# A row softmax on one core: the row maxima moved into a fallback path, eight larger tiles, two late loads on SyncE's queue

## The chip, the cores and the metric

The kernel runs on one core of one Trainium2 chip. The metric is the device time in microseconds (us) of one execution; before the change its median over 9 runs is 160.14 us (159.97 to 160.28). One execution was also taken by the hardware profiler. Its own time is 160.04 us, and its span, from the first to the last recorded instruction, is 158.7 us; the 1.34 us between the two lie outside what the profile shows.

## What is computed

A softmax with temperature 2 over the last axis of a 16 x 1024 x 512 array of float32:

```python
x_scaled = x / 2.0
x_max = np.max(x_scaled, axis=-1, keepdims=True)
exp_x = np.exp(x_scaled - x_max)
return exp_x / np.sum(exp_x, axis=-1, keepdims=True)
```

There are 16,384 rows of 512 numbers, drawn from a normal distribution. Input and output are 33.55 MB each, and each is moved once. The maximum cancels in the quotient; it is there so that the exponential can't overflow.

## The kernel before

The rows are spread over the 128 partitions of the on-chip memory, so each partition has 128 rows to do. "A row" below means one row in each partition, 262,144 bytes in all. A tile is some rows of every partition; within a tile the rows of one partition lie side by side in the main memory, so that one partition's share of a transfer is one unbroken run (a tile of 15 rows: 30,720 bytes).

The tiles are listed in `PLAN`: 3, 7, 13 and then seven times 15 rows. They live in one arena of 98 rows, in which each is computed in place. The first eight tiles fill it, and the last two (tiles 8 and 9) take the places of earlier ones: tile 8 those of tiles 0, 1 and 2, tile 9 those of tiles 2 and 3. A tile is cut into chunks of 3 to 5 rows, 27 in all.

- **Loads.** Tile 0 goes out on SyncE's queue (L105), tile 1 in three pieces on ScalarE's (L110), both ahead of the start barrier; tiles 2 to 7 follow on ScalarE's queue (L114). Tile 8 is issued by ScalarE after its exponentials of tile 4, tile 9 after those of tile 5 (`AFTER`), each when the stores of the tiles in its place have landed (L189, L190).
- **VectorE** takes the negated maximum of a chunk's rows from the loaded data (L118), and for the chunk two places back (`LAG`) the reciprocal of the row sums (L127) and the multiplication by it. In tiles 1 to 3 (`FUSED`) that is one TENSOR_TENSOR per chunk (L131), otherwise one TENSOR_SCALAR per row (L138).
- **ScalarE** takes exp(0.5 x + bias) row by row, with the row sum as a by-product. The bias is the value that VectorE left in `stats`. The rows of tiles 0 to 5 are written out one by one (L176); those of tiles 6 to 9 run in a loop of 5 rows a turn (L211), which waits on a semaphore that TensorE passes on (L168, L203).
- **SyncE** stores tile after tile (L158), each when its last chunk has been multiplied (L157), and at the end waits for the stores (L162).

Nothing plans the order at run time: each engine follows its own list and waits on semaphores. Transfers of one queue run in the order in which they were issued, and the two queues share the same 16 DMA engines.

Of the kernel before, what the change touches and what calls it, by code (L numbers as in the profile page):

```python
# [6 lines left out]

PLAN = [
    ([3], 0), ([4, 3], 3), ([5, 4, 4], 10), ([5] * 3, 23), ([5] * 3, 38), ([5] * 3, 53),
    ([5] * 3, 68), ([5] * 3, 83), ([5] * 3, 0), ([5] * 3, 15),
]
ARENA = 98
LAG = 2

SPREAD = 1

AFTER = {8: 4, 9: 5}  # L20

FUSED = {1, 2, 3}

LOOP = 6
E = 5


@with_exitstack
def kernel(
# [5 lines left out]
    nc = tc.nc  # L35
    tc.close()
    tc.compile()
    fp32 = mybir.dt.float32

    xf = x.flatten_outer_dims()  # L40
    of = out.flatten_outer_dims()
    N, D = xf.shape
    P = nc.NUM_PARTITIONS
    n_rows = N // P
    assert sum(sum(c) for c, _ in PLAN) == n_rows

    arena = nc.alloc_sbuf_tensor("arena", (P, ARENA, D), fp32)

    stats = nc.alloc_sbuf_tensor("stats", (P, n_rows), fp32)
    recip = nc.alloc_sbuf_tensor("recip", (P, n_rows), fp32)  # L50

    tiles, chunks, base = [], [], 0
    for t, (cs, at) in enumerate(PLAN):
        r = sum(cs)
        tiles.append((base, r, at))
        o = 0
        for c in cs:
            chunks.append((t, base + o, c, at + o))  # L60
            o += c
        base += r
    last_chunk = {c[0]: k for k, c in enumerate(chunks)}

    def dram(ap, t):
        b, r, _ = tiles[t]
        return ap[b * P : (b + r) * P].rearrange("(p r) d -> p r d", r=r)

    def sb(t):
        _, r, at = tiles[t]  # L70
        return arena[:, at : at + r, :]


    behind = {}
    for t, (_, r, at) in enumerate(tiles):
        for u in range(t):
            _, ru, au = tiles[u]
            if at < au + ru and au < at + r:
                behind.setdefault(t, []).append(u)

    ld = [nc.alloc_semaphore(f"ld{t}") for t in range(len(tiles))]
    awaited = sorted({u for us in behind.values() for u in us})


    st, need = {}, {}
    for t in sorted(behind):
        new = [u for u in behind[t] if u not in st]
        sem = nc.alloc_semaphore(f"st{t}")
        st.update({u: sem for u in new})
        need[t] = (sem, 16 * len(new))  # L90
    s_end = nc.alloc_semaphore("s_end")
    s_max = nc.alloc_semaphore("s_max")
    s_exp = nc.alloc_semaphore("s_exp")
    s_go = nc.alloc_semaphore("s_go")
    s_rec = nc.alloc_semaphore("s_rec")
    s_mul = nc.alloc_semaphore("s_mul")

    def issue_loads(begin, end):


        for t in range(begin, end):
            if t in behind:
                continue
            if t == 0:
                nc.sync.dma_start(out=sb(t), in_=dram(xf, t)).then_inc(ld[t], 16)  # L105
            elif t == SPREAD:

                r = tiles[t][1] - 1
                for p, q, lo, hi in ((0, P, 0, r), (0, 126, r, r + 1), (126, P, r, r + 1)):
                    nc.scalar.dma_start(  # L110
                        out=sb(t)[p:q, lo:hi], in_=dram(xf, t)[p:q, lo:hi]
                    ).then_inc(ld[t], 16)
            else:
                nc.scalar.dma_start(out=sb(t), in_=dram(xf, t)).then_inc(ld[t], 16)  # L114

    def do_max(k):
        t, b, c, a = chunks[k]
        nc.vector.reduce_max(  # L118
            out=stats[:, b : b + c],
            in_=arena[:, a : a + c],  # L120
            axis=mybir.AxisListType.X,
            negate=True,
        )._wait_ge(ld[t], 48 if t == SPREAD else 16).then_inc(s_max, 1)

    def do_mul(k):
        t, b, c, a = chunks[k]
        nc.vector.reciprocal(  # L127
            out=recip[:, b : b + c], in_=stats[:, b : b + c]
        )._wait_ge(s_exp, k + 1).then_inc(s_rec, 1)
        if t in FUSED:  # L130
            nc.vector.tensor_mul(  # L131
                out=arena[:, a : a + c],
                in0=arena[:, a : a + c],
                in1=recip[:, b : b + c].unsqueeze(2).to_broadcast([P, c, D]),
            )._wait_ge(s_rec, k + 1).then_inc(s_mul, 1)
            return
        for r in range(c):
            ins = nc.vector.tensor_scalar_mul(  # L138
                out=arena[:, a + r],
                in0=arena[:, a + r],  # L140
                scalar1=recip[:, b + r : b + r + 1],
            )
            if r == 0:
                ins._wait_ge(s_rec, k + 1)
        ins.then_inc(s_mul, 1)

    def compute_and_store():

        for k in range(len(chunks) + LAG):
            if k < len(chunks):  # L150
                do_max(k)
            if k >= LAG:
                do_mul(k - LAG)


        for t in range(len(tiles)):
            nc.sync.wait_ge(s_mul, last_chunk[t] + 1)  # L157
            nc.sync.dma_start(out=dram(of, t), in_=sb(t)).then_inc(  # L158
                st[t] if t in awaited else s_end, 16
            )  # L160

        nc.sync.wait_ge(s_end, 16 * (len(tiles) - len(awaited)))  # L162


        straight = [k for k, c in enumerate(chunks) if c[0] < LOOP]
        loop = [k for k, c in enumerate(chunks) if c[0] >= LOOP]
        for k in loop:
            nc.tensor.wait_ge(s_max, k + 1).then_inc(s_go, 1)  # L168


        nc.scalar.preload_act_table(mybir.ActivationFunctionType.Exp)  # L171
        late = sorted(behind)
        for k in straight:
            t, b, c, a = chunks[k]
            for r in range(c):
                ins = nc.scalar.activation(  # L176
                    out=arena[:, a + r],
                    in_=arena[:, a + r],
                    func=mybir.ActivationFunctionType.Exp,
                    bias=stats[:, b + r : b + r + 1],  # L180
                    scale=0.5,
                    accum_out=stats[:, b + r : b + r + 1],
                )
                if r == 0:
                    ins._wait_ge(s_max, k + 1)
            ins.then_inc(s_exp, 1)
            while late and last_chunk[AFTER[late[0]]] <= k:
                u = late.pop(0)
                nc.scalar.wait_ge(*need[u])  # L189
                nc.scalar.dma_start(out=sb(u), in_=dram(xf, u)).then_inc(ld[u], 16)  # L190
        assert not late


        first = chunks[loop[0]][1]
        assert all(
            c == E and b == first + j * E and a == b % ARENA
            for j, (_, b, c, a) in enumerate(chunks[k] for k in loop)
        )
        row = nc.scalar.alloc_register("row")
        nc.scalar.reg_mov(row, first)  # L200
        with nc.scalar.While(lambda: nc.scalar.snap(row, min_val=first, max_val=n_rows) < n_rows):
            now = nc.scalar.snap(row, min_val=first, max_val=n_rows - E)
            nc.scalar.wait_ge(s_go, 1).then_inc(s_go, -1)  # L203
            at = nc.s_assert_within(
                now % ARENA, 0, ARENA - E,
                skip_runtime_bounds_check_because="no chunk reaches over the arena's end",
            )
            for r in range(E):
                data = arena[:, r : ARENA - E + 1 + r][:, bass.ds(at, 1)]
                stat = stats[:, r : n_rows - E + 1 + r][:, bass.ds(now, 1)]  # L210
                ins = nc.scalar.activation(  # L211
                    out=data,
                    in_=data,
                    func=mybir.ActivationFunctionType.Exp,
                    bias=stat,
                    scale=0.5,
                    accum_out=stat,
                )
            ins.then_inc(s_exp, 1)
            nc.scalar.reg_add(row, row, E)  # L220

    here = str(nc.cur_bb)
    entry, rest = nc.main_func.blocks[0], list(nc.main_func.blocks[1:])
    head, jumps = entry.instructions[:-5], entry.instructions[-5:]
    entry.instructions = []
    nc.switch_bb("main", None)
    issue_loads(0, 2)
    first = list(entry.instructions)  # L230
    at = next(k for k, i in enumerate(head) if type(i).__name__ == "InstDrain")
    entry.instructions = head[:at] + first + head[at:]
    act = []
    entry.instructions = list(entry.instructions) + [i for i in jumps if i not in act]
    nc.switch_body(here, parent=None, valid_engines=[i.engine for i in jumps])
    issue_loads(2, len(tiles))
    compute_and_store()


# [28 lines left out]
```

## Time and profile before

| quantity | value |
|---|---|
| median of 9 runs | 160.14 us |
| the profiled execution: time / span | 160.04 / 158.7 us |
| bytes moved, mean rate over the span | 67.13 MB, 423 GB/s |
| VectorE busy | 131.4 us (83%), 155 instructions |
| ... of it row maxima (L118, 27) | 72.2 us |
| ... of it multiplications (L131, 8 and L138, 93) | 19.9 and 38.6 us |
| ScalarE busy | 94.4 us (59%) |
| last load landed / last store issued / its landing | 127.8 / 147.1 / 158.6 us |

The page of a profile has the busy share of each engine and of the DMA engines in 40 slices of the span, one digit a slice (9 is 90% or more); the DMA queues with their packets, megabytes and the time that their packets took as a share of 16 engines' span; and the chain of waits, which follows the work that ended last back to the start. q1 is SyncE's queue, q10 ScalarE's, and q14 fetches instructions. The view of windows gives for stretches of the span the busy time of VectorE, ScalarE and GpSimd with their instructions, TensorE's clock, the DMA share and the rate. "DVE" is VectorE, "ACT" ScalarE, "POOL" GpSimd and "SP" SyncE. Lines like L118 are those of the kernel's source.

### The profile page before, as it was taken

How to read it: one execution, taken by the hardware profiler on the slowest of the kernel's cores; microseconds unless marked ns; L12 is line 12 of the kernel's file. 1: busy time of each engine (PE TensorE's matmuls, PEld its weight loads, DVE VectorE, ACT ScalarE, POOL GpSimd, SP SyncE). 2: the span in 40 equal slices, each digit the busy share in tenths (PEclk: the TensorE clock that was granted, in tenths of full speed). 3: DMA queues.
4: the chain of work that ended last, by engine and by line, in shares of the span. 5: the costliest groups of instructions: out<-in, count | busy, mean ns of one | idle time of the engine just before them, and what ended most of it. 6: DMA issues, size and time to landing. Idle time of an engine off the chain costs nothing.

```text
span 158.7 us, 621 instructions
## 1 busy us (share of the span) xinstructions
DVE 131.4 (83%) x155; ACT 94.4 (59%) x257; POOL 0.2 (0%) x4
## 2 busy tenths in 40 slices
DVE  0467699999999999999999999996999379999000
ACT  0359297736874684679748786667566809764000
POOL 0000000000000000000000000000000000000000
DMA  7989999999999999999999999999999999999995
GB/s 274 454 362 430 427 415 465 430 386 428 466 454 395 426 463 438 418 443 418 449 418 449 418 449 418 441 426 426 441 418 449 418 449 418 449 418 449 410 457 256
DMA packets 3026, 67.13 MB, mean 423 GB/s; under 512 B 336, under 2 KB 336, under 8 KB 720
## 3 DMA queue, kind: packets, MB, share of 16 engines
q1 hardware_dynamic: 1584, 34.34, 50.5%
q10 hardware_dynamic: 1440, 32.77, 48.5%
q14 instruction: 2, 0.02, 0.0%
HBM read 33.55 MB, written 33.55 MB: 423 GB/s over the span
## 4 chain that ended last, share of the span: by engine, by line
DMA 52%; DVE 38%; issue 0%
DMA arena<-in_x_dram 38%; DVE stats L118 18%; DMA out_dram<-arena 14%; DVE arena L131 13%; DVE arena L138 7%; DVE recip L127 1%
## 5 line engine op out<-in xcount | busy, mean ns | idle before, releaser
L118 DVE TENSOR_REDUCE stats<-arena 128x5 f32<-128x2560 f32 (+2 forms) x27 | 72.2, 2677 | 14.7 <-DMA arena<-in_x_dram 14.7
L176 ACT ACTIVATE arena<-arena,stats 128x512 f32<-128x512 f32 x68 | 48.2, 711 | 23.4 <-DVE stats L118 23.4
L211 ACT ACTIVATE arena<-arena,stats x60 | 42.5, 710 | 20.7 <-ACTq L203 20.7
L138 DVE TENSOR_SCALAR arena<-arena,recip 128x512 f32<-128x512 f32 x93 | 38.6, 483 | 0.7
L131 DVE TENSOR_TENSOR arena<-arena,recip 128x2560 f32<-128x2560 f32 (+2 forms) x8 | 19.9, 2492 | 0.3
L176 ACT ACTIVATION_READ_ACCUMULATOR arena<-arena,stats 128x1 f32 x68 | 12.8, 188 | 0.0
L211 ACT ACTIVATION_READ_ACCUMULATOR arena<-arena,stats x60 | 11.2, 187 | 0.0
L171 ACT ACT_TABLE_LOAD x1 | 1.3, 1283 | 6.0 <-issue 6.0
L127 DVE RECIPROCAL recip<-stats 128x5 f32<-128x5 f32 (+2 forms) x27 | 4.8, 178 | 0.0
L252 POOL MEMSET const-uint8-127<- 128x1 uint8 x1 | 0.1, 102 | 0.0
L252 POOL MEMSET const-bfloat16-1.0<- 128x1 bf16 x1 | 0.1, 101 | 0.0
L252 POOL MEMSET const-float32-0.0<- 128x1 f32 x1 | 0.1, 98 | 0.2 <-issue 0.2
L252 POOL MEMSET const-float32-1.0<- 128x1 f32 x1 | 0.1, 98 | 0.0
## 6 DMA issues: line engine op xcount, KB each, us to landing
arena<-in_x_dram ACTq DMA_DIRECT2D x7, 3840.0 KB, 46.9
out_dram<-arena SPq DMA_DIRECT2D x7, 3840.0 KB, 22.5
arena<-in_x_dram ACTq DMA_DIRECT2D x1, 3328.0 KB, 14.5
out_dram<-arena SPq DMA_DIRECT2D x1, 3328.0 KB, 20.7
out_dram<-arena SPq DMA_DIRECT2D x1, 1792.0 KB, 17.3
arena<-in_x_dram ACTq DMA_DIRECT2D x1, 1536.0 KB
arena<-in_x_dram SPq DMA_DIRECT2D x1, 768.0 KB, 6.2
out_dram<-arena SPq DMA_DIRECT2D x1, 768.0 KB, 15.1
```

The lines of the kernel that those rows point to most:

```text
L118: nc.vector.reduce_max(out=stats[:, b : b + c], in_=arena[:, a : a + c], axis=mybir.AxisListType.X, negate=True,)._wait_ge(ld[t], 48 if t ...
L127: nc.vector.reciprocal(out=recip[:, b : b + c], in_=stats[:, b : b + c])._wait_ge(s_exp, k + 1).then_inc(s_rec, 1)
L131: nc.vector.tensor_mul(out=arena[:, a : a + c], in0=arena[:, a : a + c], in1=recip[:, b : b + c].unsqueeze(2).to_broadcast([P, c, D]),)._w ...
L138: ins = nc.vector.tensor_scalar_mul(out=arena[:, a + r], in0=arena[:, a + r], scalar1=recip[:, b + r : b + r + 1],)
L171: nc.scalar.preload_act_table(mybir.ActivationFunctionType.Exp)
L176: ins = nc.scalar.activation(out=arena[:, a + r], in_=arena[:, a + r], func=mybir.ActivationFunctionType.Exp, bias=stats[:, b + r : b + r ...
L211: ins = nc.scalar.activation(out=data, in_=data, func=mybir.ActivationFunctionType.Exp, bias=stat, scale=0.5, accum_out=stat,)
L252: nc = _bacc.Bacc("TRN2", target_bir_lowering=False, num_devices=1)
```

## The change

- **No maxima on the main path.** ScalarE takes exp(0.5 x) without a bias as soon as a tile has landed: TensorE waits for each load and gives ScalarE one count per chunk (L183 of the changed kernel).
- **A check and a general path.** When everything has been multiplied, VectorE counts the rows whose sum lies between 1 and 1e30, one matmul adds the counts of the partitions, and VectorE writes a flag. VectorE, ScalarE and GpSimd read it (L139). If a row is outside, they do everything again, 8 rows at a time, with the maximum; the DMAs of this path are GpSimd's. Otherwise they branch over it.
- **Tiles** of 3, 7, 13, 25, 25, 25, 15 and 15 rows. The first six fill the arena; tile 6 takes the places of tiles 0, 1 and 2, tile 7 takes the rest of tile 2's place and part of tile 3's.
- **Loads** of tiles 0 to 5 are issued as before (0 by SyncE, the others by ScalarE). Tiles 6 and 7 are issued by SyncE, in a fixed place among the stores: stores 0 to 3, load 6, store 4, load 7, stores 5, 6, 7.
- **ScalarE** has 23 rows written out and then a loop of 5 rows a turn for the other 105.
- **VectorE** does reciprocal and multiplication for two chunks of a tile at once (up to 10 rows), always as one TENSOR_TENSOR.

The diff, cut to its core:

```diff
-PLAN = [
-    ([3], 0), ([4, 3], 3), ([5, 4, 4], 10), ([5] * 3, 23), ([5] * 3, 38), ([5] * 3, 53),
-    ([5] * 3, 68), ([5] * 3, 83), ([5] * 3, 0), ([5] * 3, 15),
-]
+TILES = [(3, 0), (7, 3), (13, 10), (25, 23), (25, 48), (25, 73), (15, 0), (15, 15)]
+LATE = {6: (0, 1, 2), 7: (3,)}
 ARENA = 98
-LAG = 2
+HEAD = [3, 4, 3, 5, 4, 4]
+E = 5
 SPREAD = 1
-AFTER = {8: 4, 9: 5}
-FUSED = {1, 2, 3}
-LOOP = 6
-E = 5
+LO, HI = 1.0, 1.0e30
+G = 8
...
+    def load(eng, t):
+        r = tiles[t][1]
+        parts = [(0, P, 0, r)]
+        if t == SPREAD:
+            parts = [(0, P, 0, r - 1), (0, 126, r - 1, r), (126, P, r - 1, r)]
+        for p, q, lo, hi in parts:
+            eng.dma_start(
+                out=sb(t)[p:q, lo:hi], in_=dram(xf, t)[p:q, lo:hi]
+            ).then_inc(ld[t], 16)
...
+    def store(eng, t):
+        eng.wait_ge(s_mul, upto[t])
+        eng.dma_start(out=dram(of, t), in_=sb(t)).then_inc(stored_by.get(t, s_end), 16)
...
+    def rounds(eng, body, step=1):
+        last = n_rows // G
+        i = eng.alloc_register("tile")
+        eng.wait_ge(s_flag, 1)
+        eng.reg_load(i, flag[0:1, 0:1])
+        with eng.While(lambda: eng.snap(i, min_val=0, max_val=last) < last):
+            body(eng.snap(i, min_val=0, max_val=last - 1))
+            eng.reg_add(i, i, step)
+    def early():
+        load(nc.sync, 0)
+        load(nc.scalar, 1)
+    def loads():
+        for t in range(2, min(LATE)):
+            load(nc.scalar, t)
...
-    def do_max(k):
-        t, b, c, a = chunks[k]
-        nc.vector.reduce_max(
-            out=stats[:, b : b + c],
-            in_=arena[:, a : a + c],
-            axis=mybir.AxisListType.X,
-            negate=True,
-        )._wait_ge(ld[t], 48 if t == SPREAD else 16).then_inc(s_max, 1)
...
+        nc.vector.memset(ones[:, :], 1.0).then_inc(s_ones, 1)
+        for j, ks in enumerate(pairs):
+            b, c = starts[ks[0]], sum(sizes[k] for k in ks)
+            a = b % ARENA
+            nc.vector.reciprocal(
+                out=recip[:, b : b + c], in_=stats[:, b : b + c]
+            )._wait_ge(s_exp, ks[-1] + 1).then_inc(s_rec, 1)
             nc.vector.tensor_mul(
                 out=arena[:, a : a + c],
                 in0=arena[:, a : a + c],
                 in1=recip[:, b : b + c].unsqueeze(2).to_broadcast([P, c, D]),
-            )._wait_ge(s_rec, k + 1).then_inc(s_mul, 1)
-            return
-        for r in range(c):
-            ins = nc.vector.tensor_scalar_mul(
-                out=arena[:, a + r],
-                in0=arena[:, a + r],
-                scalar1=recip[:, b + r : b + r + 1],
-            )
...
+            )._wait_ge(s_rec, j + 1).then_inc(s_mul, 1)
+        nc.vector.tensor_scalar(
+            out=inside[:, :], in0=stats[:, :], scalar1=LO, scalar2=HI,
+            op0=Alu.max, op1=Alu.min,
+        ).then_inc(s_cnt, 1)
+        nc.vector.tensor_tensor(
+            out=inside[:, :], in0=inside[:, :], in1=stats[:, :], op=Alu.is_equal
+        )._wait_ge(s_cnt, 1).then_inc(s_cnt, 1)
+        nc.vector.reduce_sum(
+            out=count[:, :], in_=inside[:, :], axis=mybir.AxisListType.X
+        )._wait_ge(s_cnt, 2).then_inc(s_cnt, 1)
+        nc.vector.tensor_scalar(
+            out=flag[:, :], in0=total[:, :], scalar1=float(N), scalar2=float(n_rows // G),
+            op0=Alu.is_ge, op1=Alu.mult,
+        )._wait_ge(s_tot, 1).then_inc(s_flag, 1)
         for t in range(len(tiles)):
-            nc.sync.wait_ge(s_mul, last_chunk[t] + 1)
-            nc.sync.dma_start(out=dram(of, t), in_=sb(t)).then_inc(
-                st[t] if t in awaited else s_end, 16
-            )
...
-        for k in loop:
-            nc.tensor.wait_ge(s_max, k + 1).then_inc(s_go, 1)
...
+            nc.tensor.wait_ge(ld[t], 48 if t == SPREAD else 16).then_inc(s_go, owner.count(t))
+        nc.tensor.wait_ge(s_ones, 1)
+        nc.tensor.matmul(
+            total[:, :], lhsT=count[:, :], rhs=ones[:, :], start=True, stop=True
+        )._wait_ge(s_cnt, 3).then_inc(s_tot, 1)
+        nc.scalar.preload_act_table(Exp)
+        for k, c in enumerate(HEAD):
+            take(nc.scalar, s_go, 1)
+            for b in range(starts[k], starts[k] + c):
                 ins = nc.scalar.activation(
-                    out=arena[:, a + r],
-                    in_=arena[:, a + r],
-                    func=mybir.ActivationFunctionType.Exp,
-                    bias=stats[:, b + r : b + r + 1],
-                    scale=0.5,
-                    accum_out=stats[:, b + r : b + r + 1],
+                    out=arena[:, b], in_=arena[:, b], func=Exp, scale=0.5,
+                    accum_out=stats[:, b : b + 1],
                 )
...
-            while late and last_chunk[AFTER[late[0]]] <= k:
-                u = late.pop(0)
-                nc.scalar.wait_ge(*need[u])
-                nc.scalar.dma_start(out=sb(u), in_=dram(xf, u)).then_inc(ld[u], 16)
...
+        exponentials(straight, n_rows)
+        for t in (0, 1, 2, 3):
+            store(nc.sync, t)
+        for t, then in ((6, (4,)), (7, (5, 6, 7))):
+            nc.sync.wait_ge(s_home[t], landings(LATE[t]))
+            load(nc.sync, t)
+            for u in then:
+                store(nc.sync, u)
...
+        def gpsimd(_):
+            nc.gpsimd.wait_ge(s_end, at_end)
+            for i in range(n_rows // G):
+                nc.gpsimd.dma_start(out=data, in_=x_g[i]).then_inc(g_ld, 16)
+                nc.gpsimd.wait_ge(g_ld, 16 * (i + 1)).then_inc(g_go, 1)
+                take(nc.gpsimd, g_mul, 1)
+                nc.gpsimd.dma_start(out=o_g[i], in_=data).then_inc(g_st, 16)
+                nc.gpsimd.wait_ge(g_st, 16 * (i + 1))
...
+        rounds(nc.vector, vector)
+        rounds(nc.scalar, scalar)
+        rounds(nc.gpsimd, gpsimd, n_rows // G)
+        nc.sync.wait_ge(s_end, at_end)
```

Here `take` waits for a count and takes it off again, `exponentials` is the loop of 5 rows a turn, and the functions `vector` and `scalar` of the general path hold the maximum, exponential, reciprocal and multiplication for its 8 rows.

## The prediction

> **What bounds the kernel now.** I read the page from part 2. Times are microseconds of the profiled execution, whose span is 158.7.
>
> ```profile
> DVE  0467699999999999999999999996999379999000
> ACT  0359297736874684679748786667566809764000
> DMA  7989999999999999999999999999999999999995
> ...
> q1 hardware_dynamic: 1584, 34.34, 50.5%
> q10 hardware_dynamic: 1440, 32.77, 48.5%
> q14 instruction: 2, 0.02, 0.0%
> HBM read 33.55 MB, written 33.55 MB: 423 GB/s over the span
> ...
> DMA 52%; DVE 38%; issue 0%
> ```
>
> The DMA row never leaves 9 between the first slices and the last, and the two data queues together fill 99% of 16 engines' span. VectorE is nearly as full (83%), and the chain of waits puts 38% of the span on it. So the first question is whether VectorE makes the transfers wait anywhere. The view of windows answers it (the last two columns are the DMA share and GB/s):
>
> ```profile
> 16.00:30.00 14.00, 12.70 (x9) 8.65 (x25) 0.00 (x0) 1.00 1.03 441
> 30.00:60.00 30.00, 29.83 (x17) 19.85 (x56) 0.00 (x0) 1.00 0.99 423
> 60.00:82.00 22.00, 21.82 (x32) 14.54 (x40) 0.00 (x0) 1.00 1.02 441
> ...
> 100.00:127.70 27.70, 23.00 (x35) 18.41 (x52) 0.00 (x0) 1.00 1.00 430
> ...
> 147.00:156.00 9.00, 0.09 (x1) 0.00 (x0) 0.00 (x0) 1.00 1.01 434
> ```
>
> From 147 to 156 VectorE and ScalarE are idle and the transfers run at 434 GB/s; from 60 to 127 both work and it is 430 to 441. The engines neither slow the transfers nor leave them without work. The chain runs through VectorE only because a store waits for its multiply; that store then queues behind others. The kernel is bound by 67.1 MB at some 433 GB/s.
>
> How close it is at the end: a row of all partitions is 128 x 512 x 4 = 262,144 bytes, 0.605 at 433 GB/s, or 1.65 rows per us. 256 rows (128 in, 128 out) take 155.0, and the rest of the span, 3.7, is the start, its slow first slices (274 GB/s in the first of 4 us) and the last landing. So R rows have passed at about 3.5 + R / 1.65. All but the last store (241 rows) have passed at 149.6; the last store was issued at 147.1 (the timeline). By the packet records of the trace the first load, issued at 0.0, has data moving 1.05 later, so its deadline was about 148.5. VectorE was in time by about 1.4.
>
> **What the Trainium skill says.** "DMA: Bandwidth & Descriptors", Specifications, gives a fabric ceiling of 435 GB/s: the 430 to 441 here agree. The same page, Issuing engines are not separate DMA queues, says that transfers from SyncE, ScalarE and GpSimd share the same 16 DMA engines, so another issuer saves only issue time; here q1 alone (437 GB/s in 129 to 147) is as fast as q1 and q10 together (436 in 60 to 127). Under Queues, rings and completion order it says that an engine alternates between queues packet by packet; shares of 51.2% and 49.9% with equal packets agree. Under Why small descriptors are slow it names a fixed cost per packet, which is my largest term; I take its size from the trace.
>
> **The change part by part.**
>
> *The maxima go.* 27 TENSOR_REDUCE, 72.2 of VectorE, disappear; ScalarE waits for a load instead of a maximum (23.4 of idle time on the first 68 rows). By the windows none of it is on the transfers' path: worth 0. It moves the last store's issue away from its deadline. The multiplies become one TENSOR_TENSOR for up to 10 rows (0.565 per row by the row of 2,825 ns for 5, instead of 0.414): VectorE then has 128 x 0.565 = 72 plus 17 reciprocals, far under the span.
>
> *Is every transfer still there in time?* Count rows as above, adding the rows that must have passed.
> - Store 3 (25 rows) comes late, near 60: tile 3 must land (near 36), ScalarE takes 25 x 0.705 = 17.6, the last multiplies some 4. ScalarE's queue still holds loads 4 and 5 then: no gap.
> - Load 6 waits for stores 0 to 2 (home near 68) behind store 3, with store 3's own packets and load 5 still running. Store 4 needs tile 4 (near 58), so is ready near 81; the queue needs it after 98 loads, 48 stores and load 6 = 161 rows, at 101. Cover: 20.
> - Load 7 waits for store 3 (146 rows, near 92). Load 6 and store 4 lie queued ahead, 40 rows, 24. Nothing waits behind it but store 5, ready near 106 and needed after 201 rows at 125.
> - Load 7 has landed after 128 loads and stores 0 to 4 (73): 201 rows, 125.3. ScalarE 15 x 0.705 = 10.6; the ten-row multiply runs from 132.6 to 138.4, the five-row one to 141.4. Store 7 goes out near 141.5, deadline 148.5. Cover 7, where it was 1.4.
>
> So the transfers still run without a gap. ScalarE's six loads after the barrier (3.37) become four; it is waiting for data then: 0.
>
> *Packet length.* A packet is one partition's run. Its price, from the DMA view cut to three stages:
>
> ```profile
> q1 hardware_dynamic: 117, 0.72, 19.0%
> ...
> q1 hardware_dynamic: 117, 3.12, 45.1%
> ...
> q1 hardware_dynamic: 288, 7.86, 101.4%
> ```
>
> The first is 18 to 27, packets of 6,144 bytes: 0.190 x 16 x 9 / 117 = 233.8 ns. The second is 44 to 60, 26,624 bytes: 986.8 ns. The third is 129 to 147, 256 packets of 30,720 bytes and 32 that only signal: 1,141 ns. First and third give 27.1 bytes per ns and 7.1 ns per packet; the second then should be 989.5 and is 986.8. Each DMA engine carries 8 packets per transfer. Before, 10 tiles x 2 x 8 = 160; after, 8 x 2 x 8 = 128 (the split piece of tile 1 stays). 32 x 7.1 = 0.23 saved. Bounds: 0 (a share above 100% says that neighbouring packets overlap a little, so the fixed cost may be hidden) to 0.3. No packet of 51,200 bytes is in the trace; I extrapolate 7.1 + 51,200 / 27.1 = 1,896 ns.
>
> *Instruction fetches.* q14 shows 2 packets of 8 KB in the span, one in 60 to 127; each holds one DMA engine for 0.31 by the same formula, and the slowest engine sets the end. ScalarE's 68 written-out rows become 23 and a loop, VectorE's 155 instructions some 40, so the late one may go; GpSimd's text grows by 32 DMAs that are branched over, which may bring one back. Between -0.31 and +0.31; I take -0.15.
>
> *The added tail.* Three operations on 128 numbers, a reduction, one matmul, a flag, a register load and a branch on three engines come after the last multiply. No row shows the matmul or the register load; 5 us is a generous bound, from ten operations at about 0.2 each (the reciprocal's 178 ns) and 3 for two unknown ones. Store 7 needs about 17 from its issue to its landing, so they are hidden: 0. Without that cover they would cost their full 5. GpSimd's DMAs do not run: the sum of a row's 512 values of exp(x / 2) for x drawn from a normal distribution lies near 580, between 1 and 1e30.
>
> Sum: 0.23 + 0.15 = 0.38 less. The profiled execution took 160.04 (span 158.7 and 1.34 around it), 0.10 under the median of 160.14. From its own time 159.66; against the median **159.75**.
>
> **Rivals.**
>
> 1. *Nothing to save.* Packets' fixed cost overlaps with the neighbours and the fetches stay: 160.1. For: DMA shares of 1.01 to 1.03. Against: 6,144-byte packets are measurably slower per byte.
> 2. *Long packets run below the rate* (the slower side). For: in 8 to 17, where 13-row loads run alone, 161 packets moved only 400 GB/s; that stage has odd small pieces, yet also stretched packets. Against: at 30,720 bytes nothing of it is left. Place: the 48 packets per engine of 25-row tiles. At 1% over the extrapolation they cost 48 x 19 ns = 0.91, so 160.7; against the forecast of 159.75 the line of slower by 0.2% (160.46) is reached at 0.71 / 48 = 15 ns, a mean of 1,911 ns.
> 3. *The queue behind load 7 stalls.* SyncE's waits are now in one fixed order; if load 7 came over 7 later than counted, the last store would be late by the rest; 3 more gives 162.7. Against: covers of 20, 24 and 7.
> 4. *The maxima did slow the early transfers* and the 386 to 426 GB/s of the stages from 6 to 16 rise to 433: about 0.5 in all, so 159.2. Against: the first tiles are issued as before.
> 5. *The general path is taken*, so that the change doesn't do what it says: 16 more round trips of 67 MB in all, at least 155 more, about 315. Against: the value of the sums.
>
> **How the numbers follow.** Main case 0.50 (own range 159.5 to 159.9), rival 1 0.25, rival 2 0.15, rival 3 0.04, rival 4 0.05, rival 5 0.01. 0.2%, about what a measurement of this kernel can tell from no change, is 0.32: faster means under 159.82. Four fifths of the main case (0.40) and rival 4 give faster 0.45; the rest of the main case and rival 1 give the same 0.35; rivals 2, 3 and 5 slower 0.20. Range 159.35 to 160.8: it takes in the bounds of packets and fetches and rival 2 up to 1%, and leaves out half of rival 2, rivals 3 and 5, and most of rival 4.
>
> **What would show it.** DMA row at 9 throughout and 430 to 437 GB/s in every stage after 20; packets of 51,200 bytes at about 1,896 ns (over 1,911: rival 2); VectorE's busy time near 75 and no TENSOR_REDUCE of 128x2560; last store issued near 141; q14 with one packet or none (two or more: towards rival 1). Wrong is the forecast if a stage shows a DMA share below 0.95, or if the last store's data starts later than the end of the store before it.

## The result and the profile after

The changed kernel takes 161.20 us (median of 10 runs, 160.50 to 162.17) against 160.09 us of the kernel before on the same chip (30 runs, 159.96 to 160.28): a ratio of 1.0071, 95% interval 1.0057 to 1.0085. It is slower by some 1.1 us, and its runs spread five times as wide. Runs over 1.5% above the fastest of the same kernel count as slow and are left out of the medians below; there were two, both of the experiment that gives the kernel before the larger tiles. The profiled execution took 161.32 us with a span of 159.86; before it was 160.04 and 158.68.

The page of the changed kernel, parts 2 and 3:

```profile
DVE  0044509800298940989600689909920006970000
ACT  0675495007999069992019996598000299000000
POOL 0000000000000000000000000000000000000000
DMA  7999999989997999989999799999899999999994
GB/s 277 428 378 445 504 459 435 372 354 406 487 480 324 457 436 461 441 387 436 487 461 448 341 454 407 410 500 487 351 430 430 413 423 500 389 415 446 417 446 177
...
q1 hardware_dynamic: 1584, 42.21, 61.5%
q10 hardware_dynamic: 864, 24.90, 36.9%
q14 instruction: 2, 0.02, 0.0%
HBM read 33.55 MB, written 33.55 MB: 420 GB/s over the span
```

VectorE and ScalarE now have gaps all over; the DMA engines are as full as before, with 576 packets fewer. The rate in a single slice jumps because a packet of 51,200 bytes lasts half a slice and counts where it starts, so longer stretches have to be compared. In the view of windows (last columns DMA share and GB/s), first the kernel before, then the changed one, whose lines have two more columns ahead of VectorE's, for TensorE's matmuls and weight loads:

```profile
20.00:42.00 22.00, 21.83 (x16) 15.56 (x43) 0.00 (x0) 1.00 1.03 437
42.00:75.00 33.00, 32.79 (x31) 22.77 (x63) 0.00 (x0) 1.00 1.00 430
75.00:140.00 65.00, 59.95 (x85) 43.89 (x122) 0.00 (x0) 1.00 1.00 432
```

```profile
20.00:42.00 22.00, 0.00 (x0) 0.00 (x0) 7.55 (x4) 11.36 (x38) 0.00 (x0) 1.00 0.98 412
42.00:75.00 33.00, 0.00 (x0) 0.00 (x0) 25.16 (x10) 25.61 (x84) 0.00 (x0) 1.00 1.02 441
75.00:140.00 65.00, 0.00 (x0) 0.00 (x0) 33.26 (x17) 34.01 (x110) 0.00 (x0) 1.00 0.99 429
140.00:156.00 16.00, 0.19 (x2) 0.09 (x2) 2.73 (x5) 0.00 (x0) 0.00 (x0) 1.00 1.00 431
```

Weighted, 20 to 75 went from 433 to 429 GB/s and 75 to 140 from 432 to 429. That is slightly less with full queues, but no more than the packets at the edges of a stretch can make. SyncE's waits in the changed kernel (waiter, what it waited for, us in total, times, longest):

```profile
SPq L127 <- DVE arena L161: 108.4, 8, 26.2
SPq L111 <- DMA out_dram<-arena: 27.8, 2, 14.4
SPq L253 <- DMA out_dram<-arena: 17.6, 1, 17.6
```

SyncE waits for VectorE most of the time, but the DMA engines don't wait for SyncE: by the packet records their only pauses of more than 0.1 us after 20 us are two instruction fetches of 0.3 us on one engine each, as before. The last line is the wait for the end: the last store was issued at 141.9 and took 17.6 to land, about half of it behind the store ahead of it, whose packets ended at 150.4.

Where the time went is seen in the trace's packet records. Consecutive packets of one DMA engine follow each other within 4 ns, so the 16 engines can be told apart. I call a packet stretched by what it takes over 7 ns + bytes / 27.19 per ns, which fits nearly all of them (51,200 bytes: median 1,891 ns). In us per engine:

```
                                    before   changed   changed, another execution
time of the execution               160.04   161.32    160.55
packets without stretch             155.44   155.21    155.21
stretch, mean of the engines          1.48     2.03      2.04
  of it in packets from 20 to 42      0.26     0.59      0.57
  of it from 75 on                    0.14     0.31      0.43
last packet ends, mean              157.75   158.08    158.11
last packet ends, slowest engine    158.32   159.50    158.71
```

The span grew by 1.18: 0.33 in the mean engine, 0.85 because one engine ended 1.42 behind the mean instead of 0.57. The windows at the end show it too. In the kernel before, no data packet starts after 157.8; in the changed one the share of 0.15 after 158.1 is one last packet on one of the 16 engines:

```profile
157.80:158.30 0.50, 0.00 (x0) 0.00 (x0) 0.00 (x0) 1.00 0.00 0
```

```profile
158.10:158.60 0.50, 0.00 (x0) 0.00 (x0) 0.00 (x0) 0.00 (x0) 0.00 (x0) 1.00 0.15 61
```

The other 0.10 of the time lie outside the span. The two executions of the changed kernel have nearly the same mean end, and their slowest engines differ by 0.79, as their times do (0.77): between these two, the spread is the lateness of one engine. In the first of them that engine was set back at two places, both the eighth and last packet of a late load, behind which a store follows in SyncE's queue: load 6, ending at 101.24, 0.25 over; load 7, ending at 126.24, 0.83 over (1,962 ns for 30,720 bytes). From there the delay went to the end unchanged. In the kernel before no packet after 76 was stretched by over 0.09.

### The profile page after: what moved, and what is told of

It reads as the page before. It is cut to its first block, busy times and chain, and to the rows that moved or that the text cites. A ratio compares the mean times of both kernels' runs of the same rounds, so it can differ in the third digit from the quotient of the medians.

```text
span 159.9 us, 616 instructions
## 1 busy us (share of the span) xinstructions
PE 0.2 (0%) x2; PEld 0.1 (0%) x2; DVE 74.8 (47%) x39; ACT 80.5 (50%) x257; POOL 0.2 (0%) x4
## 5 line engine op out<-in xcount | busy, mean ns | idle before, releaser
L267 ACT ACTIVATE arena<-arena x105 | 64.4, 615 | 45.2 <-ACTq L130 45.2
L161 DVE TENSOR_TENSOR arena<-arena,recip 128x5120 f32<-128x5120 f32 (+5 forms) x17 | 71.0, 4174 | 0.6
L158 DVE RECIPROCAL recip<-stats 128x10 f32<-128x10 f32 (+5 forms) x17 | 3.4, 200 | 64.6 <-ACT arena L267 49.8
L267 ACT ACTIVATION_READ_ACCUMULATOR arena<-arena x105 | 19.7, 187 | 0.0
L193 ACT ACTIVATE arena<-arena 128x512 f32<-128x512 f32 x23 | 14.1, 614 | 5.8 <-ACTq L130 5.8
L193 ACT ACTIVATION_READ_ACCUMULATOR arena<-arena 128x1 f32 x23 | 4.3, 186 | 0.0
```

The source lines that it names most:

```text
L158: nc.vector.reciprocal(out=recip[:, b : b + c], in_=stats[:, b : b + c])._wait_ge(s_exp, ks[-1] + 1).then_inc(s_rec, 1)
L161: nc.vector.tensor_mul(out=arena[:, a : a + c], in0=arena[:, a : a + c], in1=recip[:, b : b + c].unsqueeze(2).to_broadcast([P, c, D]),)._w ...
L193: ins = nc.scalar.activation(out=arena[:, b], in_=arena[:, b], func=Exp, scale=0.5, accum_out=stats[:, b : b + 1],)
L267: ins = nc.scalar.activation(out=data, in_=data, func=Exp, scale=0.5, accum_out=stats[:, r : n_rows - E + 1 + r][:, bass.ds(now, 1)],)
```

## The experiments

Each kernel was timed beside the kernel before on the same chip; all ratios are to that. A "change" below is a place where a load is followed by a store in SyncE's queue while ScalarE's queue is empty. The changed kernel has two, behind load 6 and behind load 7; the kernel before has none.

### Which part of the change: tiles, queue, maxima

Two theories at first. M: the loads among the stores in one queue. L: the 25-row transfers.

Late loads on ScalarE's queue, the rest as changed:

```diff
-        exponentials(straight, n_rows)
+        for t, upto_row in ((6, 73), (7, 88)):
+            exponentials(done, upto_row)
+            done = upto_row
+            nc.scalar.wait_ge(s_home[t], landings(LATE[t]))
+            load(nc.scalar, t)
+        exponentials(done, n_rows)
...
+        for t in range(len(tiles)):
+            store(nc.sync, t)
...
```

> The changed kernel with tiles 6 and 7 loaded from ScalarE's queue (after its exponentials of rows 72 and 87), SyncE's queue with stores alone. Theory M (mixed queue: where a load is followed by a store in one queue and no other queue has packets, the load's last packet stretches, on one engine by up to 0.83, and that engine ends last): 159.7 to 160.1, spread under 0.4, no packet of a late load stretched by over 0.1. Theory L (the 25-row packets cost it, by stretched loads near 28 to 36): still 160.5 to 161.2.

Measured: 161.31 (160.43 to 161.70), ratio 1.0073 [1.0051, 1.0094]. Against M as stated: without any change of direction in a queue it is as slow. Eleven packets after 76 were stretched by over 0.09, seven of them of the late loads of 30,720 bytes (the worst by 0.44) taking turns with stores of 51,200; most of these were the seventh of an engine's eight packets of the load, in the changed kernel they were the eighth.

The tiles of before, late loads on SyncE's queue, the rest as changed:

```diff
-TILES = [(3, 0), (7, 3), (13, 10), (25, 23), (25, 48), (25, 73), (15, 0), (15, 15)]
-LATE = {6: (0, 1, 2), 7: (3,)}
+TILES = [(3, 0), (7, 3), (13, 10), (15, 23), (15, 38), (15, 53), (15, 68), (15, 83), (15, 0), (15, 15)]
+LATE = {8: (0, 1, 2), 9: (3,)}
...
-        for t in (0, 1, 2, 3):
+        for t in (0, 1, 2, 3, 4):
...
-        for t, then in ((6, (4,)), (7, (5, 6, 7))):
+        for t, then in ((8, (5,)), (9, (6, 7, 8, 9))):
```

> The changed kernel with the tiles of before (3, 7, 13, seven of 15), the two late loads still on SyncE's queue behind stores 4 and 5. Theory M: slow as the changed kernel, 160.6 to 161.5, spread over 0.8, stretched last packets of the two late loads. Theory L: 159.9 to 160.3.

Measured: 160.38 (160.22 to 160.84), 1.0018 [1.0010, 1.0027]; run again in a later set, 160.65 (160.27 to 161.15), 1.0030 [1.0018, 1.0042]:

> The run with 15-row tiles and late loads on SyncE's queue once more, on the chip of the other two, as their line to compare with: 160.2 to 160.8 by all theories.

Between the theories: about half or more of the loss is gone with the tiles, not all of it.

The kernel before with its two late loads moved to SyncE's queue and nothing else:

```diff
             nc.sync.dma_start(out=dram(of, t), in_=sb(t)).then_inc(
                 st[t] if t in awaited else s_end, 16
             )
+            u = t + 4
+            if u in behind:
+                nc.sync.wait_ge(*need[u])
+                nc.sync.dma_start(out=sb(u), in_=dram(xf, u)).then_inc(ld[u], 16)
...
-            while late and last_chunk[AFTER[late[0]]] <= k:
-                u = late.pop(0)
-                nc.scalar.wait_ge(*need[u])
-                nc.scalar.dma_start(out=sb(u), in_=dram(xf, u)).then_inc(ld[u], 16)
...
```

> The kernel before with nothing changed but its two late loads issued by SyncE (behind stores 4 and 5) and no longer by ScalarE. Theory M: 160.6 to 161.5 with a wide spread. Theory L: 160.0 to 160.2, as before.

Measured: 160.63 (160.33 to 160.89), 1.0036 [1.0023, 1.0049]. So the move costs 0.5 with tiles and maxima as before; with the queue, the loads' place among the stores changed too (issued at 74.0 and 88.8 instead of 62.7 and 81.5). In its trace the last packets of both late loads are stretched, up to 0.33 and 0.60.

The tiles of before and late loads on ScalarE's queue, of the change only the missing maxima and the general path:

> The changed kernel with the tiles of before and the late loads on ScalarE's queue: of the change, the missing maxima and the general path alone. Both theories: 160.0 to 160.2, no change. If it is under 159.8, the maxima did cost transfers something; if over 160.4, the general path or the wider multiplies cost something.

Measured: 162.97 (161.55 to 163.19), 1.0165 [1.0137, 1.0194], which no theory had. The windows of its profile (161.91 us) around the issue of the last store, and the line of that store in the timeline (start, duration):

```profile
147.00:149.00 2.00, 0.00 (x0) 0.00 (x0) 2.00 (x2) 0.00 (x0) 0.00 (x0) 1.00 0.61 261
149.00:151.00 2.00, 0.19 (x2) 0.09 (x2) 0.93 (x5) 0.00 (x0) 0.00 (x0) 1.00 0.57 246
```

```profile
149.10 0.33 SPq L127 DMA_DIRECT2D out_dram<-arena  x1
```

Here the DMA engines do run out of work: the last store leaves at 149.1, past the 148.5 that the prediction had worked out. Without maxima the stores start earlier (11.3, before 14.8) and take their turns with the loads from then on, and the last load lands at 133.8, where before it had landed by 127.8; the last 15 rows with their multiplies of 10 and 5 follow. So I multiplied the last tile in three steps of 5 rows:

```diff
-        if pairs and len(pairs[-1]) == 1 and owner[pairs[-1][0]] == t:
+        if pairs and len(pairs[-1]) == 1 and owner[pairs[-1][0]] == t and t != 9:
```

> The run with 15-row tiles and late loads on ScalarE's queue (162.97), the last tile multiplied in three single steps of 5 rows in place of 10 and 5: the last store leaves about 2.2 earlier. If that run was long because its last store came after the one before had drained: 160.1 to 161.0. If something else made it long: 162.5 to 163.2.

Measured: 160.37 (160.13 to 160.62), 1.0019 [1.0010, 1.0028]; in its profile the last store left at 147.8. So the 2.6 are the late store's. What stays is 0.3 for the missing maxima with the general path; this kernel's stores, too, run close to their deadline, so the 0.3 is not free of it.

The kernel before, maxima kept, with the new tile sizes, its late loads after rows 57 and 82:

```diff
-    ([3], 0), ([4, 3], 3), ([5, 4, 4], 10), ([5] * 3, 23), ([5] * 3, 38), ([5] * 3, 53),
-    ([5] * 3, 68), ([5] * 3, 83), ([5] * 3, 0), ([5] * 3, 15),
+    ([3], 0), ([4, 3], 3), ([5, 4, 4], 10), ([5] * 5, 23), ([5] * 5, 48), ([5] * 5, 73),
+    ([5] * 3, 0), ([5] * 3, 15),
...
-AFTER = {8: 4, 9: 5}
+AFTER = {6: 58, 7: 83}
...
```

> The kernel before, with its maxima, with the tile sizes of the change (three of 25 rows in place of five of 15), late loads still on ScalarE's queue. Theory L (the 25-row transfers set the engines apart, about 0.8 of the loss): 160.6 to 161.3, engine ends spread over 1.0. Theory S (only the order of late loads and stores matters): 160.0 to 160.3.

Measured: 163.79 (four runs, 162.47 to 164.81), 1.0244 [1.0193, 1.0296]. More than either theory. The windows of its profile (162.93 us):

```profile
42.00:75.00 33.00, 32.76 (x30) 21.83 (x60) 0.00 (x0) 1.00 1.01 431
75.00:105.00 30.00, 29.79 (x45) 22.17 (x62) 0.00 (x0) 1.00 1.00 410
...
151.00:153.00 2.00, 0.06 (x1) 0.00 (x0) 0.00 (x0) 1.00 0.58 246
```

Two losses: the last store left at 151.1, too late, and from 75 to 105 the rate fell to 410 with full engines. There stores of 51,200 bytes took turns with late loads of 30,720; 51 of 160 such stores were stretched by 0.09 to 0.59, and 26 of 128 loads by up to 1.07. The tiles of 25 rows don't suit the old order at all, so this run measures more than the tiles.

### Is it the length of the packets?

In the next runs each transfer of a 25-row tile goes out as two DMAs one behind the other, so its packets are 26,624 and 24,576 bytes.

```diff
+        if r == 25 and True:
+            parts = [(0, P, 0, 13), (0, P, 13, 25)]
...
+        for lo, hi in [(0, 13), (13, 25)] if r == 25 and True else [(0, r)]:
+            eng.dma_start(out=dram(of, t)[:, lo:hi], in_=sb(t)[:, lo:hi]).then_inc(
...
```

Where only the loads or only the stores are split, one of the two `True` is `False`.

> The changed kernel, each transfer of a 25-row tile issued as two DMAs of 13 and 12 rows, one after the other in the same queue: same tiles, same waits, packets of 26,624 and 24,576 bytes in place of 51,200. If the length of the packet is the cause: 160.2 to 160.5, as with 15-row tiles. If it is the size of the tile (when transfers become ready and who runs beside whom): 160.9 to 161.5.

Measured: 160.83 (160.79 to 161.24), 1.0053 [1.0040, 1.0066]. Loads alone, and stores alone:

> As the run with split 25-row transfers, but only the loads are split, the stores keep packets of 51,200 bytes. If long load packets are the cause (stretched loads near 28 to 36): 160.2 to 160.6. If long store packets are: 160.9 to 161.5.

Measured: 160.57 (160.50 to 162.01), 1.0034 [1.0021, 1.0047].

> The changed kernel with only the stores of the 25-row tiles split in 13 and 12 rows, the loads keep 51,200-byte packets. If long load packets are the cause (loads alone split gave 160.57): 160.9 to 161.5. If any shortening helps alike: 160.4 to 160.8.

Measured: 160.99 (160.56 to 161.87), 1.0069 [1.0048, 1.0091]. The runs with loads alone and stores alone came out as forecast if the long load packets are the cause. But splitting loads and stores together gave no more than the loads alone (160.83 and 160.57, intervals that overlap), and none of the three is back at the kernel before. Then with each part a block of its own in the main memory, of 13 and 12 rows and of 15 and 10 (here 15 and 10):

```diff
+    CUT = [(0, 15), (15, 25)]
+    def part(ap, t, lo, hi):
+        b, r, _ = tiles[t]
+        return ap[(b + lo) * P : (b + hi) * P].rearrange("(p r) d -> p r d", r=hi - lo)
...
```

> As the run with 25-row transfers split in 13 and 12 rows (160.83), but each part is a block of its own in the main memory, so that the step from one partition's run to the next is 26,624 or 24,576 bytes and no longer 51,200; packets, tiles and waits as there. If the step of 51,200 bytes is what collides with the late loads' 30,720: 160.2 to 160.5, no stretched packets near 99. If only packet length and order matter: 160.7 to 161.1.

Measured: 160.91 (160.66 to 161.52), 1.0059 [1.0045, 1.0074].

> As the run before it with blocks of 15 and 10 rows: most transfers, the late loads among them, then have the same step and packet of 30,720 bytes, as in the kernel before. If equal lengths of what runs side by side keep the engines in step: 160.1 to 160.4, below the 13 and 12 run. If not: as that run, within 0.2.

Measured: 161.10 (160.70 to 161.16), 1.0060 [1.0047, 1.0073]. This one has the packets and steps in memory of the run with 15-row tiles and is nearly as slow as the changed kernel, measured beside it:

> The changed kernel itself, on the chip of the other three runs of this set: 160.5 to 162.2, ratio near 1.007. All theories say the same; it is the line to compare with.

Measured: 161.37 (160.33 to 162.03), 1.0084 [1.0051, 1.0116]. These differences have to be read with the price of the added packets: splitting both ways adds 48 packets per engine, 0.34 us at 7 ns each, and splitting one way 0.17. Without that, the split kernels lose 0.4 to 0.8 against the kernel before, where the changed kernel loses 1.1 to 1.3. So the length of the packets can account for a part of the loss, but not for all of it, and the place in memory made no visible difference (0.82 and 0.85 over the kernel before). The last try in this direction gave each block its own wait, so that work starts per 15 or 10 rows; the order of the transfers stayed:

> The changed kernel with each 25-row tile made two tiles of 15 and 10 rows, in the same order of transfers: the packets and places in memory of the run with blocks of 15 and 10 (161.1), but a load wakes ScalarE, and a store leaves, per 15 or 10 rows. If the grain of the waits (late first stores, then 25 rows at once) is what costs: 160.2 to 160.6. If the places of the late loads among the stores cost: 160.9 to 161.3.

Measured: 160.94 (160.69 to 161.19), 1.0052 [1.0039, 1.0065]; so the grain of the waits is not it either. This kernel's first late load ended at 99.7, while ScalarE's queue was busy until 103.2, so it has one change only; its packets after 76 are stretched by 0.16 at most, but those from 20 to 42 by 0.55 per engine more than in the kernel before. So most of its loss of 0.86 has another cause.

### The change from load to store

Loads 6 and 7 one behind the other after store 4, so that one change is left:

```diff
-        for t in (0, 1, 2, 3):
+        for t in (0, 1, 2, 3, 4):
             store(nc.sync, t)
-        for t, then in ((6, (4,)), (7, (5, 6, 7))):
+        for t in (6, 7):
             nc.sync.wait_ge(s_home[t], landings(LATE[t]))
             load(nc.sync, t)
-            for u in then:
-                store(nc.sync, u)
+        for u in (5, 6, 7):
+            store(nc.sync, u)
```

> The changed kernel with loads 6 and 7 one behind the other after store 4, so that only load 7 is followed by a store. Theory M (a load's last packet stretches where a store follows it in the only busy queue): stretched packets at the end of load 7 alone, none at the end of load 6; time a little lower, 160.6 to 161.2. Rival (it is the late loads' place in memory): both loads' last packets stretch, 161.1 to 161.5.

Measured: 160.42 (15 runs, 160.18 to 161.17), 1.0028 [1.0016, 1.0039]: less than theory M had forecast, and the stretched packets where it had them. In the packet records the end of load 6, now followed by a load, has no stretched packet; the end of load 7 has one, by 0.55, on the engine that then ends last. Both loads together ahead of store 4, 15 us earlier:

> The changed kernel with loads 6 and 7 one behind the other ahead of store 4, so again only load 7 is followed by a store, and the last store leaves some 15 earlier. Theory M (each change from a load to a store in the only busy queue costs some 0.3 to 0.8 on the slowest engine): as with both loads behind store 4 (160.42), 160.2 to 160.7, stretched packets only at the end of load 7. If the time of the last store mattered: below 160.2.

Measured: 160.49 (22 runs, 160.15 to 162.40), 1.0033 [1.0019, 1.0047]. Nine packets at the end of load 7 are stretched, the worst by 0.86, and apart from two small ones at the start of load 6 (0.14 and 0.21) none elsewhere after 76. The same with 15-row tiles:

> The run with 15-row tiles (160.38, 160.65) with its two late loads one behind the other after store 4: one change from load to store in place of two. Theory M: 160.1 to 160.4, lower than with two. Without M: as before, 160.4 to 160.65.

Measured: 160.31 (22 runs, 160.04 to 160.51), 1.0008 [1.0002, 1.0015]: the best of the variants, and still not below the kernel before (160.12 beside it). In its profile no packet is stretched at the end of a load. The other way, four changes: loads 6 and 7 in pieces of 8 and 7 rows, stores 4 and 5 in pieces of 5 and 20, taking turns.

```diff
+        for t, u in ((6, 4), (7, 5)):
+            nc.sync.wait_ge(s_home[t], landings(LATE[t]))
+            for (a, b), (c, d) in (((0, 8), (0, 5)), ((8, 15), (5, 25))):
+                nc.sync.dma_start(out=sb(t)[:, a:b], in_=dram(xf, t)[:, a:b]).then_inc(ld[t], 16)
+                half(u, c, d)
...
```

> The changed kernel with loads 6 and 7 cut in 8 and 7 rows and stores 4 and 5 cut in 5 and 20 rows, the pieces taking turns: four changes from load to store in place of two, bytes and tiles the same; the packets added are 32 per engine, 0.2. Theory M: two more changes cost another 0.4 to 1.6, so 161.8 to 163. Without M: 161.3 to 161.6.

Measured: 161.94 (161.11 to 162.52), 1.0110 [1.0088, 1.0133]. The page of this kernel and that of the 15-row tiles with loads together, part 2, show the end of the span:

```profile
DMA  7999999989799979999999899999899998999993
GB/s 275 433 369 442 489 444 457 439 344 506 308 491 501 416 329 415 508 501 408 408 421 421 383 390 428 446 483 438 363 407 435 463 483 387 405 477 398 468 398 130
```

```profile
DMA  7999999999999999999999999999999999999995
GB/s 263 451 376 448 447 411 374 421 452 432 420 455 456 408 449 410 457 410 457 410 457 410 457 410 457 410 457 410 457 403 465 403 465 395 467 403 465 395 472 256
```

The last slice falls from 256 to 130 GB/s (the changed kernel has 177): with four changes the slowest engine ends 2.00 after the mean, with two 1.42 in the profile first shown, with one and small tiles 0.38. With four changes the stretched packets near the ends of the load pieces are the fifth to the eighth of eight, not the last alone.

All by number of changes, difference to the kernel before beside it, us:

```
changes        0        1              2              4
25-row tiles   +1.22**  +0.34 +0.37    +1.11 +1.31    +1.82
15-row tiles   +0.36*   +0.19          +0.29 +0.57    -
15-row tiles, maxima kept              +0.54          -
*  late loads on ScalarE's queue, last store near its deadline
** late loads on ScalarE's queue, taking turns with stores of 51,200 bytes
```

The kernels with split transfers and the two whose last store came too late are not in this table.

Of the +1.82, some 0.2 are the 32 packets that cutting added per engine. With the late loads in SyncE's queue, the row of the 25-row tiles is the clearest: taking one of two changes away brought 0.7 to 1.0, wherever the two loads stood, and adding two cost 0.5 to 0.7. With 15-row tiles the step from two changes to one is hardly clear of noise. The entry without a change shows that this is not the only way to lose as much, and the 15-row tiles with two changes show that the tiles matter as much as the changes. It isn't the same amount each time; a likely reason is that what counts is how far one engine is set back behind the others, not what all lose.

## Why the prediction was wrong

*What bounds the kernel* held: the transfers, and not the engines that compute; removing 72.2 of VectorE's work brought nothing, and VectorE's busy time came out at 74.8 (counted near 75).

*Every transfer in time* held: load 6 issued at 72.6 (counted near 68), load 7 at 92.3 (92), store 4 at 78.6 (81), the last store at 141.9 (141.5), the tail of check and flag over by 143.1, 1.2 after the last multiply (5 allowed). The deadline of 148.5 was right too: the run whose last store left at 149.1 lost time by it, the one at 147.8 hardly. So rival 3, a stall in the queue's fixed order, did not happen, nor did rival 5. Rival 4 fell too: the stretch of packets before 20 was 0.99 per engine with maxima and 1.12 without.

*Packet length* held in size: 155.44 to 155.21, the 0.23 saved, and 1,891 ns where 1,896 was extrapolated. Rival 2 named the right direction and half of the loss (160.7), with the wrong mechanism: packets of 51,200 bytes run at full rate, with a median of 1,891 ns where it needed 1,911.

*Fetches*: two packets of q14, as before. The 0.15 taken for this term did not come. (The sum itself is 160.14 - 0.38 = 159.76, not 159.75.)

*The step that failed* is "so the transfers still run without a gap" taken as "so the rate stays", and below it the reading that "q1 alone (437 GB/s in 129 to 147) is as fast as q1 and q10 together". That stretch has stores alone. The trace before had no place where a load is followed by a store in the only busy queue, so the cost of this was unknown, and I had not bounded it: it should have stood in the sum with a range. The sum has the late loads among SyncE's stores at nothing, because their cover was wide. The runs showed that in this order of transfers they set single engines back (0.25 and 0.83 in the profiled execution), and the last store lands with the slowest engine. Taking away one of the two changes gave back 0.7 to 1.0 of the 1.1 to 1.3. The larger tiles were put at nothing but their packets, too, and with the tiles of before 0.5 to 1.0 came back. So the two don't simply add up: most is lost where both meet, and moving the late loads to ScalarE's queue did not help there (161.31).

The forecast's own signs could not show this. The share stayed at 0.98 or more in every stage shown, and the last store's data followed without a pause: a stretched packet counts as busy. Beside the fetches, only the rate of 430 to 437 after 20 failed (412 from 20 to 42).

The sentence of the Trainium skill ("DMA: Bandwidth & Descriptors", Issuing engines are not separate DMA queues) that another issuer only saves issue time, which I leaned on, was too narrow a ground for this: the measured difference here (0.5 for the kernel before with its two late loads moved) is not issue time.

What stays open: what stretches a load's last packets; why 15-row tiles lose less per change (at the first of their two, no packet was stretched by over 0.09); why late loads on ScalarE's queue beside 25-row stores are as slow as the changed kernel, without any change within a queue (packets of 51,200 and 30,720 bytes taking turns are stretched there, and far more in the run with the old order and new tiles, while equal packets taking turns in the kernel before are not); and the 0.1 to 0.55 more of stretched packets from 20 to 42, which all kernels without maxima show and the two profiled variants with them do not (it is 0.23 in the kernel of 15-row tiles that loses 0.36). No run isolated these.

## What to carry to other kernels

When 16 DMA engines are full for the whole span, a full DMA row says nothing about the last half per cent: compare the mean end of the engines with the end of the slowest, and be wary when runs spread more than before. Give a place where a load is followed by a store in the only busy queue a price of its own, and try the late loads one behind the other: here one such place less was worth 0.7 to 1.0 with 25-row tiles. In the kernel before, late loads in a queue of their own were better by 0.5; beside 25-row stores they were not, so this has to be measured. Freeing an engine makes its stores earlier; where they took turns with loads, the last load landed later, and the last store left later, so count that deadline again.

## What the runs showed of the hardware

- The last packet of a load of 30,720 bytes, followed by a store in the same queue with no other queue busy, took up to 2,001 ns instead of 1,138, on up to fifteen of the engines and in two places on none, differently in each execution; where a load followed it instead, it did not.
- A delay of one engine was carried to the end: every engine moves eight packets of each transfer, and in the changed kernel and in the one with both loads behind store 4 the engine set back by 0.83 and 0.55 ended last.
- A packet of 51,200 bytes (1,891 ns) costs the same per byte as one of 30,720 (1,138 ns) to within 0.3%.
- Two queues take turns by packet, so the one with longer packets gets the larger share: from 18 to 27 us of the kernel before, 111 packets of one queue moved 3.07 MB beside 117 of the other with 0.72.
- With 15-row tiles and without maxima the first store left at 11.3 instead of 14.8, and the last load landed at 133.8 instead of 127.8. That the stores pushed the loads back fits this; no run isolated it.
